# Feed-forward of a hybrid decoder block: down-projection terms behind later slots, and the last four down pages split whole into pages of their own

## The chip, the cores and the metric

One core of a Trainium2 chip runs the whole program. The metric is the device time of one execution in microseconds; the median of three runs is compared. One further execution was profiled, and all rows below come from it.

## The reference, cut to what matters

One decoder layer on x of 256 rows by 1024 columns, float32: a mixer (attention branches, gates, an output projection) and then a feed-forward part. The change is in the feed-forward part:

```python
h = rms_norm(x, norm_ffn_pre_g[l])
f = (jax.nn.silu(h @ w_gate[l]) * (h @ w_up[l])) @ w_down[l]
x = x + rms_norm(f, norm_ffn_post_g[l])
```

w_gate and w_up are 1024 x 2816, w_down is 2816 x 1024. In blocks of 128 there are 22 feed-forward blocks f and two row tiles t of 128 rows.

## The kernel before

**Products in three matmuls.** Every float32 factor is split into a high part (ScalarE copies it to a shorter float, line 183) and a low part (VectorE subtracts, line 186), and a product is three matmuls, high by high, high by low, low by high (`mm3`, lines 213 to 217). A weight granule is a page of 128 x 1024; its split takes one ScalarE and one VectorE instruction when it is done whole, and two of each when it is done in halves (`split_part`, `job_split`). Its parts are `whi` and `wlo` from a ring of five buffers (WB), or, for names in `place`, pages of their own (`wextra`). Raw weights land in a ring of seven tiles (`wraw`, RB) or, for the W units, in numbered pages (`wpage`).

**Units.** The first four blocks (NAT) are computed directly: gate, then up in eight slots (`nat_slots`). The other eighteen come in six UNITS by turns: R units of two blocks, at 4, 10 and 16, and W units of four blocks, at 6, 12 and 18. An R unit has eight slots, four granules by two row tiles. A W unit computes four blocks by a scheme with seven products instead of eight: granules 21, 11, T2, T1, T3, 22, T4, two slots each. Its T granules are sums of weight pages (`job_add`, line 267, VectorE): T3, T1 and T2, two halves each, are the six early sums (`early_sums`), done during the R unit before; T4 comes in the W unit. The T slots use S, sums of the activations that VectorE and ScalarE make once in nine steps (`s_step`). All slots here have six matmuls of 512 columns or as much.

**From f to the output.** When a unit's activations are done (`done`, line 1115 and 1117, in R; `q1` to `q7`, lines 1058 to 1091, in W), `f_T` transposes them on TensorE (line 992) into the PSUM bank t, ScalarE copies the high part of fT (line 997), and one slot later VectorE subtracts the low part (line 999). The bank t has one buffer, so the next transposes wait for that subtraction. Each f then gives two down-projection slots (`z_slots`), whose matmuls accumulate in `acc` and `pv`. The terms of a unit's blocks stand in the unit after it. The last four blocks, 18 to 21, are the tail: `z_tail` makes four slots for row tile 0 and four for row tile 1, and norm and output follow.

**What sets the order.** Three things, all in program order. First, the list `slots` (from line 1142): in each unit the first part a, the transposes `left` of the unit before, the part b, the down slots `zs` of the unit before, the part c. For R these are slots 1 to 2, 3 to 4 and 5 to 8; for W 21, then 11, then T2 to T4 and the transposes of row tile 0. In the last unit two of the four down slots stand after c. Second, the list of `jobs` (lines 244 to 330), splits and sums in the order in which ScalarE and VectorE do them. Third, `run` (line 338): before each slot it emits all jobs up to the last one that the slots ahead need, at most six slots ahead and at most four new granules (`granules_ahead`, line 353). Work after a slot (`post`, and steps of `active`) is emitted between, so activations queue behind the splits that were emitted before them. SP issues each load when its ring tile or page is released (`load_raws`), in order too. Pages are handed out first freed, first used (`free`).

**The tail before.** The splits of granules 18 to 21 are eight halves, first all first halves, then all second halves (line 328); 18 and 19 go into the ring, 20 and 21 into four free pages (`in_free`, line 853).

Of the kernel before, what the change touches and what calls it, by code (L numbers as in the profile page):

```python
# [21 lines left out]
F32R = mybir.dt.float32r  # L22
# [5 lines left out]
P = 128  # L28
D = 1024
S = 256  # L30
NT = S // P
# [4 lines left out]
NFF = DFF // P  # L36
# [29 lines left out]
def tile_hybrid_block(  # L66
# [182 lines left out]
            extra.append((("gn", kc), HALF[j]))  # L249
    for kc in range(2, 4):  # L250
        job_split(("gn", kc), nr["gn", kc], (0, 1))
    for kc in range(4):
        job_split(("un", kc), nr["un", kc], None if kc else (0, 1))

# [26 lines left out]
    def units_before(i):  # L283
# [4 lines left out]
        kb, fb = UNITS[i - 1]  # L288
        return list(range(fb, fb + (4 if kb == "W" else 2)))

    for ui, (kind, f0) in enumerate(UNITS):
        ds = [lambda i=i: job_split(("d", i), dr[i]) for i in units_before(ui)]
        if kind == "R":
            rr = [raw_of([(slice(0, 256), rows(w_gate, 2 * kc * P, 2, f0 * P, 256)),
                          (slice(256, 512), rows(w_up, 2 * kc * P, 2, f0 * P, 256))], 2) for kc in range(4)]
            rs = [lambda kc=kc: job_split(("r", f0, kc), rr[kc]) for kc in range(4)]
            ad = early_sums(UNITS[ui + 1][1])
            if ui == 0:
                sjobs = [raw_of([], 2, "page") for i in range(4)]

                def s_jobs(*ns):
                    def f():
                        if ns[0] == 0:
                            touch_s()
                        for n in ns:
                            add_job(lambda n=n: s_step(n))
                    return [f]

                def touch_s():
                    use(*sjobs)  # L310

                todo = s_jobs(0) + rs[0:1] + s_jobs(1) + rs[1:2] + s_jobs(2, 3) + ds[0:1] + s_jobs(4, 5) + ds[1:2] + \
                    s_jobs(6) + ds[2:3] + s_jobs(7, 8) + ds[3:4] + ad[0:1] + rs[2:3] + ad[1:3] + rs[3:4] + ad[3:]
            else:
                n = len(ds)
                todo = rs[0:2] + [x for i in range(n) for x in ds[i:i + 1] + ad[i:i + 1]] + rs[2:3] + ad[n:n + 1] + \
                    rs[3:4] + ad[n + 1:]
        else:
            b = wsum[f0]
            sp = {n: [lambda n=n, i=i: job_split((n, f0, i), b[n][i]) for i in range(2)]  # L320
                  for n in ("11", "21", "22", "T1", "T2", "T3", "T4")}
            t4 = [lambda i=i: job_add(b["T4"][i], b["T2"][i], b["21"][i]) for i in range(2)]
            todo = sp["21"] + sp["11"] + ds[0:1] + t4[0:1] + ds[1:2] + t4[1:2]
            for n in ("T2", "T1", "T3", "22", "T4"):
                todo += sp[n]
        for f in todo:
            f()
    for h in range(2):
        for f in range(NFF - NTAIL, NFF):
            job_split(("d", f), dr[f], (h,))  # L330

# [19 lines left out]
    def granules_ahead(slots, n, most):  # L353

        def f(i):
            j, seen = i + 1, set()
            while j < len(slots) and j - i <= most:
                seen |= {x for x, _ in slots[j]["need"]} - {x for x, _ in slots[i]["need"]}
                if len(seen) > n:
                    break  # L360
                j += 1
            return j - i - 1
        return f
# [184 lines left out]
    def ev_q(base):  # L548
        def f(c, a):
            q = work.tile([P, S], F32, tag="qf", name="q", bufs=2)  # L550
            nc.vector.tensor_tensor(q, a, R1, op=OP.mult)  # L551
            qhl = work.tile([P, 2, S], F32R, tag="q", name="q", bufs=5)
            qT[base + c] = (qhl[:, 0, :], qhl[:, 1, :])
            split(q, *qT[base + c])
        return f
# [294 lines left out]

    place[("z", 7)] = z7
    place[("gn", 0)], place[("gn", 1)] = in_pages(10, 11), in_pages(12, 13)
    for f in range(NFF - 2, NFF):
        place[("d", f)] = in_free

    sig(0)
# [128 lines left out]
    def f_T(fvs, f0, n, tag="t"):  # L985

        def pe():
            b = ps(tag)
            w = [(i, t, j) for i, t in enumerate(fvs) for j in range(n)]
            for i, t, j in w:  # L990
                c = (i * n + j) * P
                nc.tensor.transpose(b[:, c:c + P], fvs[t]()[:, j * P:(j + 1) * P], ident)
            h, l = [work.tile([P, 512], F32R, tag="q", name="fT", bufs=5) for _ in range(2)]
            for i, t, j in w:
                c = (i * n + j) * P
                fT[f0 + j, t] = [v[:, c:c + P] for v in (h, l)]
            nc.scalar.activation(h, b, AF.Copy)
            yield
            nc.vector.tensor_tensor(l, b, h.bitcast(F32), op=OP.subtract)  # L999

        def start():
            th = pe()
            next(th)
            active.append(th)
        return dict(pe=start, need=[], short=True)
# [36 lines left out]
    def unit_W(f0):  # L1042
        st = {}

        def bank(n):
            if n not in st:
                st[n] = ps("s")
            return st[n]

        def slots_of(n, bk, a, start, stop, post):  # L1050
            return [dict(pe=lambda kp=kp: block(bank(bk), a, n, f0, kp, start, stop), need=[((n, f0, kp), 0)],
                         post=[lambda: active.append(post())] if kp else []) for kp in range(2)]

        def q2():
            return
            yield

        def q1():
            s1 = work.tile([P, 512], F32, tag="ph0", name="s1", bufs=1)
            nc.scalar.activation(s1, st["a"], AF.Copy)  # L1060
            yield
            g = st["g0"] = work.tile([P, 512], F32, tag="e", name="g0", bufs=4)
            nc.vector.tensor_tensor(g, st["b"], s1, op=OP.add)
            yield
            nc.scalar.activation(g, g, AF.Silu, scale=rs2[:, 0:1])

        def q6():
            st["s2"] = work.tile([P, 512], F32, tag="ph0", name="s2", bufs=1)
            nc.scalar.activation(st["s2"], st["a"], AF.Copy)
            yield  # L1070

        def q5():
            st["v5"] = work.tile([P, 512], F32, tag="pl0", name="v5", bufs=1)
            nc.scalar.activation(st["v5"], st["b"], AF.Copy)
            yield

        def q7():
            nc.vector.tensor_tensor(st["v5"], st["v5"], st["a"], op=OP.subtract)  # L1078
            yield

        def q3():
            u = st["f0"] = work.tile([P, 512], F32, tag="e", name="f0", bufs=4)
            nc.vector.tensor_tensor(u, st["b"], st["s2"], op=OP.subtract)
            nc.vector.tensor_tensor(u, u, st["g0"], op=OP.mult)
            yield

        def q4():
            g = st["f1"] = work.tile([P, 512], F32, tag="e", name="f1", bufs=4)
            nc.scalar.activation(g, st["a"], AF.Silu, scale=rs2[:, 1:2])
            yield  # L1090
            nc.vector.tensor_tensor(g, g, st["v5"], op=OP.mult)

        head = slots_of("21", "b", A(0, 1), True, True, q2)
        body = slots_of("11", "a", A(0, 0), True, True, q1), [
            s for x in (("T2", "a", R_(1), False, True, q6), ("T1", "b", R_(0), True, True, q5),
                        ("T3", "a", R_(2), False, True, q7), ("22", "b", R_(3), False, True, q3),
                        ("T4", "a", A(1, 1), False, True, q4)) for s in slots_of(*x)]
        body[1].append(f_T({0: lambda: st["f0"]}, f0, 4))
        return head, body[0], body[1], [f_T({1: lambda: st["f1"]}, f0, 4)]

    def unit_R(f0):
        st = []
# [10 lines left out]
        def done(t):  # L1113
# [4 lines left out]

        sl = [dict(pe=lambda kc=kc, t=t: pe(kc, t), need=[(("r", f0, kc), 0)],
                   post=[lambda t=t: active.append(done(t))] if kc == 3 else []) for kc in range(4) for t in range(NT)]  # L1120
        return sl[0:2], sl[2:4], sl[4:8], [f_T({t: (lambda t=t: st[t]["f"]) for t in range(NT)}, f0, 2)]

    def nat_slots():
        def pe(kc, t):
# [20 lines left out]
        slots[t - NT]["post"] = [lambda t=t: nat_mul(t)]  # L1145
    left = [f_T({t: lambda t=t: fgs[t]}, 0, 4, "pv" if t else "t") for t in range(NT)]
    for i, (kind, f0) in enumerate(UNITS):
        a, b, c, nxt = unit_W(f0) if kind == "W" else unit_R(f0)
        zs = [s for f in units_before(i) for s in z_slots("d", f, f_of, NFF - 1)]
        if i == len(UNITS) - 1:  # L1150
            slots += a + left + b + zs[0:2] + c + zs[2:4] + nxt
        else:
            slots += a + left + b + zs + c
        left = nxt
    tail = list(range(NFF - NTAIL, NFF))
    t0 = z_tail("d", tail, f_of, 0, NFF - 1)
    t1 = z_tail("d", tail, f_of, 1, NFF - 1)
# [17 lines left out]
    t1[1]["post"] = [lambda: norm3(1)]  # L1175
    t1[2]["post"] = [lambda: pn[1][0](1)]
    t1[3]["post"] = [lambda: finish(1)]
    slots += t0 + t1
    run(slots, granules_ahead(slots, WB - 1, 6))
    order.__exit__(None, None, None)  # L1180

# [22 lines left out]
```

## Time and profile before

| | |
|---|---|
| median of 3 runs | 400.02 us (399.06 to 400.92) |
| profiled execution | 402.57 us |
| its span | 400.8 us |
| mean granted TensorE clock | 0.982 of full |
| VectorE, ScalarE busy | 78%, 59% of the span |
| feed-forward slots, from the first up-projection matmul to the last matmul | about 203 to 394.7 us of the span |

The profiled execution lies above the three runs. Times of rows are microseconds from the span's start. A matmul's end is modelled, so the shown idle time ahead of a matmul is counted from that end; the distance of two starts counts all of it.

### The profile page before, as it was taken

The page shows a single profiled execution, that of the slowest core. Times are in us where ns is not written, and L with a number is a line of the kernel's source. Part 1 is how long each engine was busy: PE and PEld are TensorE (multiplying, and loading weights), DVE is VectorE, ACT ScalarE, POOL GpSimd, SP SyncE. Part 2 cuts the span into 40 slices and gives each one's busy share as a digit, 9 for nine tenths or more (in the row PEclk, how much of TensorE's full clock was granted, in tenths as well). Part 3 has the DMA queues.
Part 4 walks back from the last instruction along what each step waited for, and adds up shares of the span by engine and source line. Part 5 has one row for each costly group of instructions (what it writes and reads, how often), then busy time and mean ns, then how long its engine had stood idle before and what let it go on. Part 6 is the DMA issues. An engine that isn't in the chain of part 4 may idle for free.

```text
span 400.8 us, 6146 instructions
## 1 busy us (share of the span) xinstructions
PE 376.9 (94%) x2212; PEld 326.6 (81%) x2212; DVE 312.0 (78%) x556; ACT 235.6 (59%) x435; POOL 31.5 (8%) x51
## 2 busy tenths in 40 slices
PE   6999999999999999999999898998989989979693
PEld 4799989999999999998888677877868868756583
DVE  2699787999987577895787999689786898668724
ACT  3875675787665855653693455854465554628411
POOL 0099500000001000000000000000000000000000
PEclk9899999999999999999999999999999999989979
DMA  6969655252545744783399836666464753000002
GB/s 193 389 218 328 199 177 164 71 187 88 172 145 160 253 134 141 251 267 111 115 330 341 279 111 194 200 216 186 138 202 135 235 194 121 0 0 1 2 1 105
DMA packets 37857, 67.65 MB, mean 169 GB/s; under 512 B 2993, under 2 KB 15298, under 8 KB 37826
## 3 DMA queue, kind: packets, MB, share of 16 engines
q1 hardware_dynamic: 37826, 67.26, 51.4%
q8 instruction: 17, 0.28, 0.3%
q14 instruction: 14, 0.11, 0.1%
HBM read 66.20 MB, written 1.05 MB: 168 GB/s over the span
## 4 chain that ended last, share of the span: by engine, by line
PE 75%; DVE 11%; issue 5%; DMA 4%; ACT 4%; SPq 1%; DVEq 0%; POOLq 0%; ACTq 0%
PE acc L217 13%; PE acc L215 12%; PE acc L216 12%; PE s L215 7%; PE s L216 7%; PE s L217 7%; DVE wlo L186 5%; PE acc L612 4%; DMA wraw<-in_w_in_dram 3%; ACT whi L183 2%; PE pv L216 2%; PE pv L217 2%; PE pv L215 2%; DVE wpage L267 2%; DVE fT L999 1%
## 5 line engine op out<-in xcount | busy, mean ns | idle before, releaser
L186 DVE TENSOR_TENSOR wlo<-wraw,whi 128x512 fp32r<-128x512 f32 (+1 forms) x141 | 119.2, 868 | 29.4 <-ACT whi L183 29.1
L183 ACT ACTIVATE whi<-wraw 128x512 fp32r<-128x512 f32 (+1 forms) x140 | 101.6, 763 | 43.4 <-PE acc L216 14.5
L215 PE MATMUL acc<-hTh,whi 128*128 128x256 f32 x256 | 73.2, 286 | 0.4 <-DVE q L551 0.4
L217 PE MATMUL acc<-hTh,wlo 128*128 128x256 f32 x256 | 71.9, 281 | 0.0
L216 PE MATMUL acc<-hTl,whi 128*128 128x256 f32 x256 | 71.8, 281 | 0.0
L186 DVE TENSOR_TENSOR wlo<-wpage,whi 128x1024 fp32r<-128x1024 f32 x42 | 50.0, 1220 | 18.5 <-ACT whi L183 18.5
L183 ACT ACTIVATE whi<-wpage 128x1024 fp32r<-128x1024 f32 x42 | 43.5, 1058 | 29.3 <-PE pv L217 18.8
L215 PEld LDWEIGHTS acc<-hTh,whi 128*128 128x128 f32 x256 | 48.3, 189 | 0.7 <-DVE q L551 0.6
L216 PEld LDWEIGHTS acc<-hTl,whi 128*128 128x128 f32 x256 | 48.3, 189 | 0.0
L217 PEld LDWEIGHTS acc<-hTh,wlo 128*128 128x128 f32 x256 | 48.2, 188 | 0.0
L215 PE MATMUL s<-whi,h2h 128*128 128x512 f32 x92 | 37.6, 409 | 0.9 <-DVE v L1078 0.6
L217 PE MATMUL acc<-whi,fT 128*128 128x512 f32 (+1 forms) x80 | 30.6, 382 | 7.6 <-DVE fT L999 7.6
L216 PE MATMUL s<-wlo,h2h 128*128 128x512 f32 x92 | 36.4, 396 | 0.0
L217 PE MATMUL s<-whi,h2l 128*128 128x512 f32 x92 | 36.4, 395 | 0.0
L215 PE MATMUL acc<-whi,fT 128*128 128x512 f32 (+1 forms) x80 | 30.1, 377 | 0.0
L216 PE MATMUL acc<-wlo,fT 128*128 128x512 f32 (+1 forms) x80 | 30.0, 375 | 0.0
L267 DVE TENSOR_TENSOR wpage<-wpage 128x1024 f32<-128x1024 f32 x24 | 28.9, 1216 | 0.0
L217 PEld LDWEIGHTS acc<-whi,fT 128*128 128x128 f32 x80 | 15.6, 195 | 12.7 <-DVE fT L999 10.2
L215 PEld LDWEIGHTS s<-whi,h2h 128*128 128x128 f32 x92 | 17.3, 188 | 6.0 <-DVE fr L1117 1.6
L875 POOL TENSOR_TENSOR rs_r<-rs_e,mhalf 128x1 f32<-128x1 f32 x4 | 2.2, 546 | 241.1 <-DVE rs_e L874 241.1
L217 PEld LDWEIGHTS s<-whi,h2l 128*128 128x128 f32 x92 | 17.3, 188 | 4.2
L216 PEld LDWEIGHTS s<-wlo,h2h 128*128 128x128 f32 x92 | 17.3, 188 | 3.4
(267 smaller groups left out, 768.5 us busy)
## 6 DMA issues: line engine op xcount, KB each, us to landing
wraw<-in_w_in_dram SPq DMA_DIRECT2D x37, 512.0 KB, 4.9
wraw<-in_w_down_dram SPq DMA_DIRECT2D x22, 512.0 KB, 3.4
wpage<-in_w_up_dram SPq DMA_DIRECT2D x12, 512.0 KB, 4.1
wpage<-in_w_gate_dram SPq DMA_DIRECT2D x12, 512.0 KB, 4.1
wraw<-in_w_out_dram SPq DMA_DIRECT2D x8, 512.0 KB, 3.3
wraw<-in_w_gate_dram SPq DMA_DIRECT2D x12, 256.0 KB, 2.9
wraw<-in_w_up_dram SPq DMA_DIRECT2D x12, 256.0 KB, 3.9
wraw<-in_w_branch_a_dram SPq DMA_DIRECT2D x4, 512.0 KB, 4.3
```

What stands on the lines that cost most here:

```text
L183: nc.scalar.activation(hi, src, AF.Copy)
L186: nc.vector.tensor_tensor(lo, src, hi.bitcast(F32), op=OP.subtract)
L215: nc.tensor.matmul(dst, lh, rh, start=start, stop=False, **kw)
L216: nc.tensor.matmul(dst, lh, rl, start=False, stop=False, **kw)
L217: nc.tensor.matmul(dst, ll, rh, start=False, stop=stop, **kw)
L267: nc.vector.tensor_tensor(dst["flat"], a["flat"], b["flat"], op=OP.add)
L612: nc.tensor.matmul(acc[t], l[:, k, ts_], r, start=k == 0 and n == 0, stop=k == KT - 1 and n == 2)
L875: nc.gpsimd.tensor_tensor(r[:, 0:1], e, mhalf, op=OP.pow)
L999: nc.vector.tensor_tensor(l, b, h.bitcast(F32), op=OP.subtract)
```

## The change

The up-projection splits 1 to 3 move from the list of early jobs into the first unit, by turns with the S steps. In an R unit the six slots 3 to 8 follow the transposes `left` at once; then come three down slots, the R unit's own transposes `tr`, and the other down slots. In a W unit the down slots follow 21 and 11. The jobs are put in the same order: in an R unit splits of r and d by turns with the early sums (`braid`); in the first unit the two T2 sums (`rest`) wait until the W unit. The last four down granules are split whole, in order, and all four go into eight free pages; granules with a place of their own no longer count for the four granules of look-ahead. In the tail the last transposes come after the first of the eight slots. The ring tagged q has six buffers instead of five.

```diff
@@ -249,8 +249,7 @@
-    for kc in range(4):
-        job_split(("un", kc), nr["un", kc], None if kc else (0, 1))
+    job_split(("un", 0), nr["un", 0], (0, 1))
@@ -287,6 +286,23 @@
+    def braid(a, b):
+
+        n, o = len(a), []
+        for i in range(n):
+            o += a[i:i + 1] + b[len(b) * i // n:len(b) * (i + 1) // n]
+        return o
@@ -296,38 +312,25 @@
             ad = early_sums(UNITS[ui + 1][1])
             if ui == 0:
...
-                todo = s_jobs(0) + rs[0:1] + s_jobs(1) + rs[1:2] + s_jobs(2, 3) + ds[0:1] + s_jobs(4, 5) + ds[1:2] + \
-                    s_jobs(6) + ds[2:3] + s_jobs(7, 8) + ds[3:4] + ad[0:1] + rs[2:3] + ad[1:3] + rs[3:4] + ad[3:]
+                uns = [lambda kc=kc: job_split(("un", kc), nr["un", kc]) for kc in range(1, 4)]
+                todo = uns[0:1] + s_jobs(0) + uns[1:2] + s_jobs(1) + uns[2:3] + s_jobs(2, 3, 4, 5) + rs[0:2] + \
+                    s_jobs(6) + rs[2:3] + s_jobs(7, 8) + rs[3:4] + braid(ds, ad[0:4])
+                rest = ad[4:]
             else:
-                n = len(ds)
-                todo = rs[0:2] + [x for i in range(n) for x in ds[i:i + 1] + ad[i:i + 1]] + rs[2:3] + ad[n:n + 1] + \
-                    rs[3:4] + ad[n + 1:]
+                todo = braid(rs + ds, ad)
+                rest = []
...
-            todo = sp["21"] + sp["11"] + ds[0:1] + t4[0:1] + ds[1:2] + t4[1:2]
+            todo = sp["21"] + sp["11"] + rest[0:1] + ds[0:1] + t4[0:1] + rest[1:2] + ds[1:2] + t4[1:2]
...
-    for h in range(2):
-        for f in range(NFF - NTAIL, NFF):
-            job_split(("d", f), dr[f], (h,))
+    for f in range(NFF - NTAIL, NFF):
+        job_split(("d", f), dr[f])
@@ -355,7 +358,7 @@
-                seen |= {x for x, _ in slots[j]["need"]} - {x for x, _ in slots[i]["need"]}
+                seen |= {x for x, _ in slots[j]["need"] if x not in place} - {x for x, _ in slots[i]["need"]}
@@ -549,7 +552,7 @@
-            qhl = work.tile([P, 2, S], F32R, tag="q", name="q", bufs=5)
+            qhl = work.tile([P, 2, S], F32R, tag="q", name="q", bufs=6)
@@ -850,7 +853,7 @@
-    for f in range(NFF - 2, NFF):
+    for f in range(NFF - NTAIL, NFF):
         place[("d", f)] = in_free
@@ -990,7 +993,7 @@
-            h, l = [work.tile([P, 512], F32R, tag="q", name="fT", bufs=5) for _ in range(2)]
+            h, l = [work.tile([P, 512], F32R, tag="q", name="fT", bufs=6) for _ in range(2)]
@@ -1096,7 +1099,7 @@
-        return head, body[0], body[1], [f_T({1: lambda: st["f1"]}, f0, 4)]
+        return head + body[0], body[1], [f_T({1: lambda: st["f1"]}, f0, 4)]
@@ -1118,7 +1121,7 @@
-        return sl[0:2], sl[2:4], sl[4:8], [f_T({t: (lambda t=t: st[t]["f"]) for t in range(NT)}, f0, 2)]
+        return sl, [f_T({t: (lambda t=t: st[t]["f"]) for t in range(NT)}, f0, 2)]
@@ -1145,13 +1148,14 @@
     for i, (kind, f0) in enumerate(UNITS):
-        a, b, c, nxt = unit_W(f0) if kind == "W" else unit_R(f0)
         zs = [s for f in units_before(i) for s in z_slots("d", f, f_of, NFF - 1)]
-        if i == len(UNITS) - 1:
-            slots += a + left + b + zs[0:2] + c + zs[2:4] + nxt
+        if kind == "R":
+            sl, tr = unit_R(f0)
+            slots += sl[0:2] + left + sl[2:] + zs[0:3] + tr + zs[3:]
+            left = []
         else:
-            slots += a + left + b + zs + c
-        left = nxt
+            a, b, left = unit_W(f0)
+            slots += a + zs[0:2] + (zs[2:] + b if i < len(UNITS) - 1 else b + zs[2:])
@@ -1175,7 +1179,7 @@
-    slots += t0 + t1
+    slots += t0[0:1] + left + t0[1:] + t1
```

## Rows read from the trace of the kernel before

**Rows 1.** Part 1 of the page: busy time, share of the span, instructions.

```profile
PE 376.9 (94%) x2212; PEld 326.6 (81%) x2212; DVE 312.0 (78%) x556; ACT 235.6 (59%) x435; POOL 31.5 (8%) x51
```

**Rows 2.** Timeline at the second wait for fT: start, length, instruction, idle before.

```profile
245.91 0.40 PE L215 MATMUL acc<-whi,fT 128*128 128x512 f32 x1
246.14 0.40 PE L216 MATMUL acc<-wlo,fT 128*128 128x512 f32 x1
...
246.90 0.68 DVE L999 TENSOR_TENSOR fT<-t,fT 128x512 fp32r<-128x512 f32 x1
...
247.64 0.50 PE L217 MATMUL acc<-whi,fT 128*128 128x512 f32 x1 [1.10 <-DVE fT L999]
...
247.98 0.40 PE L215 MATMUL acc<-whi,fT 128*128 128x512 f32 x1
```

**Rows 3.** Waits of TensorE in 214 to 395 us: total, times, longest.

```profile
PE acc L217 <- DVE fT L999: 7.6, 6, 2.6
PE t L992 <- DVE fT L999: 5.4, 3, 3.5
PE s L215 <- DVE v L1078: 0.6, 1, 0.6
PE s L215 <- DVE fr L1117: 0.4, 1, 0.4
```

**Rows 4.** Timeline ahead of the longest wait for fT, TensorE, VectorE and ScalarE.

```profile
347.69 0.69 PE L992 MATMUL t<-ident,fr 128*128 128x128 f32 x4
347.81 1.22 DVE L267 TENSOR_TENSOR wpage<-wpage 128x1024 f32<-128x1024 f32 x1
...
348.85 0.58 ACT L997 ACTIVATE fT<-t 128x512 fp32r<-128x512 f32 x1
...
351.21 2.35 DVE L186 TENSOR_TENSOR wlo<-wpage,whi 128x1024 fp32r<-128x1024 f32 x2
...
353.48 0.68 DVE L999 TENSOR_TENSOR fT<-t,fT 128x512 fp32r<-128x512 f32 x1
...
354.22 0.50 PE L217 MATMUL acc<-whi,fT 128*128 128x512 f32 x1 [2.58 <-DVE fT L999]
```

**Rows 5.** Busy time by stretch: window, its us, engines (instructions), granted clock, DMA.

```profile
214.00:380.00 166.00, 152.22 (x709) 121.74 (x707) 136.21 (x140) 91.97 (x109) 0.00 (x0) 0.99 0.46 146
...
355.00:359.00 4.00, 4.00 (x15) 3.42 (x14) 0.30 (x1) 1.00 (x1) 0.00 (x0) 0.57 0.00 0
380.00:386.20 6.20, 5.91 (x17) 4.80 (x18) 0.93 (x2) 0.60 (x1) 0.00 (x0) 0.52 0.00 0
```

**Rows 6.** Timeline of the tail, TensorE and VectorE.

```profile
371.02 0.69 DVE L1084 TENSOR_TENSOR f<-f,g 128x512 f32<-128x512 f32 x1
...
373.41 0.60 PE L992 MATMUL t<-ident,f 128*128 128x128 f32 x4
...
375.33 1.29 DVE L186 TENSOR_TENSOR wextra<-wraw,wextra 128x512 fp32r<-128x512 f32 x2 [2.42 <-ACT wextra L183]
...
376.51 0.28 PE L217 MATMUL pv<-whi,fT 128*128 128x256 f32 x1
...
379.56 0.68 DVE L999 TENSOR_TENSOR fT<-t,fT 128x512 fp32r<-128x512 f32 x1
380.29 1.12 PE L992 MATMUL t<-ident,f 128*128 128x128 f32 x4 [3.50 <-DVE fT L999]
```

**Rows 7.** Timeline of TensorE in the second stretch of low clock.

```profile
382.06 0.63 PE L217 MATMUL acc<-whi,fT 128*128 128x512 f32 x1
...
382.49 0.63 PE L215 MATMUL acc<-whi,fT 128*128 128x512 f32 x1
```

**Rows 8.** A page load, the sum that uses it, and part 6 of the page.

```profile
288.84 3.20 SPq L164 DMA_DIRECT2D wpage<-in_w_up_dram  x2
...
323.75 1.22 DVE L267 TENSOR_TENSOR wpage<-wpage 128x1024 f32<-128x1024 f32 x1
...
wpage<-in_w_up_dram SPq DMA_DIRECT2D x12, 512.0 KB, 4.1
```

**Rows 9.** Waits of ScalarE in 214 to 395 us: total, times, longest.

```profile
ACT whi L183 <- PE pv L217: 23.9, 12, 5.2
```

More of the change, by code (lines that the diff above doesn't have):

```diff
@@ L289, in units_before, with s_jobs, f @@
         return list(range(fb, fb + (4 if kb == "W" else 2)))
+    sjobs = [raw_of([], 2, "page") for i in range(4)]
+    def s_jobs(*ns):
+        def f():
+            if ns[0] == 0:
+                use(*sjobs)
+            for n in ns:
+                add_job(lambda n=n: s_step(n))
+        return [f]
+    def braid(a, b):
[3 more added lines that the diff above has]
+        return o
     for ui, (kind, f0) in enumerate(UNITS):
@@ L298, in tile_hybrid_block @@
             if ui == 0:
[L299 to L310, printed above, removed]
-                todo = s_jobs(0) + rs[0:1] + s_jobs(1) + rs[1:2] + s_jobs(2, 3) + ds[0:1] + s_jobs(4, 5) + ds[1:2] + \
-                    s_jobs(6) + ds[2:3] + s_jobs(7, 8) + ds[3:4] + ad[0:1] + rs[2:3] + ad[1:3] + rs[3:4] + ad[3:]
-            else:
-                n = len(ds)
-                todo = rs[0:2] + [x for i in range(n) for x in ds[i:i + 1] + ad[i:i + 1]] + rs[2:3] + ad[n:n + 1] + \
-                    rs[3:4] + ad[n + 1:]
+                uns = [lambda kc=kc: job_split(("un", kc), nr["un", kc]) for kc in range(1, 4)]
+                todo = uns[0:1] + s_jobs(0) + uns[1:2] + s_jobs(1) + uns[2:3] + s_jobs(2, 3, 4, 5) + rs[0:2] + \
+                    s_jobs(6) + rs[2:3] + s_jobs(7, 8) + rs[3:4] + braid(ds, ad[0:4])
+                rest = ad[4:]
+            else:
+                todo = braid(rs + ds, ad)
+                rest = []
         else:
```

## Prediction

> **What bounds the kernel now.** I read the page first, then the waits of TensorE, the timeline at the waits, and the timeline of VectorE just ahead of them. The page shows TensorE busy for 94% of the span [rows 1], and where nothing waits a 128x512 matmul starts every 0.23 us [rows 2]. So time can only come from stretches where matmuls stop or where the clock is low. The feed-forward stage from 214 to 395 us has both. Its waits [rows 3] are six for the low part of fT at the first down-projection matmul that needs it (7.6 us), three at the transposes (5.4 us, the longest 3.5) and two small ones (0.6 and 0.4 us).
>
> Why fT is late is seen on VectorE. In the worst case the copy of the high part is done at 349.4, one microsecond after the transposes, but VectorE, which works in order, has 2 sums and 3 splits queued ahead of the subtraction that makes the low part, and runs them without a gap from 347.81 to 353.48 [rows 4]. The two slots between the transposes and the first term give it only 2.8 us. VectorE is not full: in 214 to 380 us it is busy 136.2 of 166 us [rows 5]. The work stands in the wrong order.
>
> **The sum, step by step.** It is made against the profiled execution: 402.57 us, a span of 400.8 and 1.8 around it. That is 2.55 above the median of the runs shown, 400.02, and above the highest of them.
>
> 1. Down-projection terms later. In a unit of kind R the transposes stay behind slot 2, but six projection slots of 1.40 us (six matmuls of 0.233), not two, now stand between them and the first term: 8.4 us instead of 2.8. In a unit of kind W the own transposes of the R before it come after three term slots, and five term slots and four slots of the unit follow: 12.6 us. The latest low part in [rows 4] comes 6.4 us after its transposes begin (347.69 by the matmul chain, 354.16 by the end of the subtraction), so both covers hold, and all six waits go. Their size: the view counts idle from a modelled end, 0.40 us after the start, while the stream starts one every 0.233, so each costs 0.17 more (246.14 to 247.64 is 1.50, that is 1.27 lost for 1.10 shown), and the next start after a wait takes 0.34 instead of 0.23 [rows 2]: 7.6 + 6 x 0.17 + 6 x 0.1 = 9.2 us.
>
> 2. The R unit's multiply. The last R slots were followed by the W unit, whose bank they hold (0.4 us shown [rows 3]); now the term slots stand between. With the same two corrections 0.7 us goes.
>
> 3. The tail. Now the eight half splits of the last four pages stand on ScalarE behind the silu that waits for the last T4 matmul, and on VectorE six of them, 3.8 us, ahead of the multiply and the subtraction for which the transposes at 380.29 wait [rows 6]. After the change the four whole splits need no buffer of the ring of five, look-ahead no longer counts them, and they are emitted up to six slots ahead. The transposes also move behind the first tail slot, 1.4 us. The wait of 3.5 goes; by starts it is 3.78 less 0.12: 3.7 us. Half splits cost two of 0.61 each on VectorE, whole ones 1.13 [rows 4, 6], which is hidden work and worth nothing.
>
> 4. What the tail pays. Two whole splits, 2.3 us, come to stand ahead of the two multiplies that make f0. The second of these ran at 371.02, so the f0 transposes at 373.41 had 1.7 us to spare (371.71 to 373.41) [rows 6]. So these wait 0.6, with the restart 0.7 us. Two more splits, the last multiply and the subtraction then end at 374.0 + 2.3 + 0.6 + 0.7 = 377.6 on the old clock, while the third matmul of the first tail slot comes 0.6 + 2.8 + 0.5 after 374.0, at 377.9: it just holds, 0.3 us to spare. Bounds of this step: 0 if the splits go still earlier, 3.0 if all four stand ahead.
>
> 5. The clock. The granted clock is 0.57 of full in 355 to 359 us and 0.52 in 380 to 386.2 [rows 5], which is the lower level, 1.2 GHz, for nearly all of it; matmuls then start every 0.43 us instead of 0.233 [rows 7]. Ahead of each fall TensorE had stood, for 2.58 us (to 354.22, [rows 4]) and for 3.5; in the stretch of the other five waits, 5.0 us together, the mean stays high enough (0.99 to 380 us with the first fall in it) for no third fall. With steps 1 and 3 both go. Low from 355.24 to 358.7 and from 380.3 to 386.1: 9.3 us, of which (0.43 - 0.233) / 0.43 = 46% is lost: 4.2 us, 1.5 and 2.7. The Trainium skill, "TensorE: Matmul & The Clock Gate", Part 1 and its terms, says that the throttled state is the default which activity lifts, and that the loss is the throttled time by one minus the ratio; by it this term would be 4.7 instead of 4.2. The trace agrees on the direction.
>
> 6. Edits costed at nothing. The first unit's `un` splits, the S steps and the last two T2 sums only change order: VectorE does the same number of splits and sums. In the first 22 us after 203 TensorE has eight up-projection and eight R slots, 22.4 us, and VectorE's three `un`, four r splits and four whole S steps (11 x 1.13) plus four half ones and two multiplies (6 x 0.6) are 16.0 us. For a later pair R and W: 24 splits and 8 sums at 1.13 and some 10 small ones come to 42 us, TensorE's 204 matmuls of 512 columns and 12 transposes to 49. That is the cover, 7 us a pair; if it is gone, rival (a) has the price. A sixth q buffer only adds room. POOL has nothing to do in the stage [rows 5]. On SP's queue the ring loads of `un` and r now precede the d loads, and the two 21 pages precede T2, which is no load; pages are issued early: the pair at 288.84 is used by the sum at 323.75 [rows 8]. The other two waits at the transposes, (5.4 - 3.5) / 2 = 0.95 us each, keep what stands ahead of them, a split and the multiply ahead of the subtraction, and stay, as does the 0.6 at T4 [rows 3].
>
> Sum: 9.2 + 0.7 + 3.7 + 4.2 - 0.7 = **17.1 us**. From the profiled time 385.5. From the median 382.9 if all runs have these losses, more if the 2.55 us by which the profiled one is longer are part of the low clock. I take the middle, **384.5 us**.
>
> **Rivals.** (a) VectorE becomes the bound. Its 29.8 us of idle time in 214 to 380 [rows 5] must shrink to some 17. For it: VectorE is dense for 6.4 us in [rows 4], and the tail has 0.3 us to spare. Against: the cover of step 6. If only half can be squeezed, half the sum comes: about 392.5 us.
>
> (b) The ring of five split buffers is what makes fT late. ScalarE waits 23.9 us, 12 times, for a down-projection matmul to free one [rows 9]. Then moving slots leaves the six waits and the first low-clock stretch where they are, and only the tail (3.7 + 2.7 - 0.7 = 5.7) comes: 401.3, the middle of median and profiled time, less 5.7, 395.5 us. The Trainium skill, "Perfetto Trace Analysis", Optimization Strategy, holds that the same gap repeating on the engine that should be full can mean too few buffers. Against: ahead of the latest subtraction VectorE waited for nothing for 5.7 us [rows 4].
>
> (c) The tail doesn't come early, because the eight free pages that its splits need are freed by this same unit's splits of 11, T2, T1 and T3. Pages are handed out first freed first, and between the split that frees the last of them, T3, and the one that takes it stand the four of 22 and T4 and three of the tail, some 8 us of VectorE at 1.13 each, so I hold it unlikely. The price is steps 3 and 4 and the second low stretch: 384.5 + 5.7, about 390 us.
>
> (d) Slower: a sum blocked on a page load. From the second R unit on, sums follow the second r split at once; on an engine in order a sum that waits for its page holds all splits and fT behind it. A page takes 4.1 us from issue to landing [rows 8]. It decides from five such waits on (5 x 4.1 is over 17.1); with all eight sums of one R and W pair (six early, two T4), 33 us less 17, it gives some 417 us. Against: the 30 us lead of [rows 8].
>
> **How the numbers follow.** My forecast has a chance of 0.72, (a) 0.12, (c) 0.08, (b) 0.05, (d) 0.03. The range 381.5 to 391 holds the forecast with its unknowns (the median taken whole, and up to 3 us for step 4, and 4.2 for the clock) and (c), and leaves out (b), (d) and most of (a). A measurement here can tell about 0.5%, 2 us, from no change. All cases but (d) are faster by more, with a little left for several small mishaps: 0.95 faster, 0.02 the same, 0.03 slower.
>
> **What would show it.** Right: the wait of the down-projection for fT is gone from TensorE's waits, that at the transposes is near 2.5 us, with one of 0.6 near the end; the granted clock is 1.0 from the stage's begin to the last matmul; VectorE's idle time in the stage is about 17 us; wextra is split in four whole pairs ahead of the last f0 multiply. Wrong: matmuls that wait for wlo (a), the fT wait still there (b), the last transposes still waiting over 2 us (c), sums that wait for a DMA (d), or the low clock at another place.

## The result, and the profile after

The changed kernel takes **383.69 us** (median of 4, 383.51 to 383.90) against 400.25 for the kernel before: 16.6 us less, a ratio of 0.959 with a 95% interval of 0.957 to 0.961. The forecast was 384.5 in a range of 381.5 to 391.

The profiled execution of the changed kernel takes 383.57 us with a span of 381.8, which is 19.0 below the profiled execution before. Of these, 17.3 lie between the first feed-forward matmul on h2 and the last matmul (190.90 to 394.43 before, 189.19 to 375.42 after). The other 1.7 lie ahead of the feed-forward part, where the change does nothing of note: the profiled execution before had a low clock in its first 20 us (mean 0.91 by its windows, 1.00 after). It fits that this is part of the 2.55 us by which it lay above the median.

TensorE's waits after the change, to be held against [rows 3] (total, times, longest; 214 to 376 us):

```profile
PE t L995 <- DVE fT L1002: 1.9, 2, 1.0
PE s L215 <- DVE v L1081: 0.6, 1, 0.6
PE t L995 <- DVE f L1087: 0.6, 1, 0.6
PE s L215 <- DVE g L1066: 0.2, 1, 0.2
```

The first row of [rows 3], 7.6 us for fT at the down-projection, is gone, and so is the R unit's multiply. The two waits at the transposes and the one at T4 are what the prediction left standing. The third row here is the price that step 4 named; the fourth, 0.2 us for g in a W unit, is new and was not forecast.

The page's first part and its clock line (granted clock in 40 slices):

```profile
PE 369.8 (97%) x2212; PEld 323.1 (85%) x2212; DVE 311.1 (81%) x552; ACT 233.7 (61%) x431; POOL 31.6 (8%) x51
...
PEclk9999999999999999999999999999999999999998
```

Busy time in the stage, with the granted clock, which answers to [rows 5]:

```profile
214.00:366.00 152.00, 148.69 (x713) 121.38 (x712) 132.15 (x131) 88.29 (x104) 0.00 (x0) 1.00 0.49 159
```

About the same work (713 matmul instructions, 709 before) takes 14 us less, the granted clock of the window is 1.00, and VectorE's idle time fell from 29.8 to 19.9 us, not quite to the 17 that the prediction gave as a sign. From 190 us to the last matmul no stretch has a low clock either (mean 1.00). The subtraction that makes the low part of fT now has room to spare. After the last R unit, TensorE, VectorE and TensorE again:

```profile
328.56 0.60 PE L995 MATMUL t<-ident,fr 128*128 128x128 f32 x4
...
328.76 1.22 DVE L266 TENSOR_TENSOR wpage<-wpage 128x1024 f32<-128x1024 f32 x1
...
329.90 2.35 DVE L186 TENSOR_TENSOR wlo<-wpage,whi 128x1024 fp32r<-128x1024 f32 x2
332.17 0.68 DVE L1002 TENSOR_TENSOR fT<-t,fT 128x512 fp32r<-128x512 f32 x1
...
342.02 0.39 PE L217 MATMUL acc<-whi,fT 128*128 128x512 f32 x1
```

VectorE still has work queued ahead of the subtraction, one sum and two splits where [rows 4] has two and three, and the low part is done 4.3 us after the transposes begin, not 6.5. But the matmul that needs it comes 13.5 us after them, 9.2 us after the low part is done (332.17 + 0.68 to 342.02). So two things changed, the queue and the place of its reader. The later place is enough by itself on these numbers: even behind a W unit's transposes the first matmul that can need the low part comes 9.4 us after they begin (265.68 to 275.04), which is over the old 6.5. The shorter queue alone is not quite enough: in the order before, the reader would have come 3.8 us after the transposes without its wait (354.22 - 2.58 - 0.17 - 347.69), half a microsecond before 4.3. No run tried the two apart.

The tail, which answers to [rows 6], with ScalarE's copies of the four pages:

```profile
354.75 3.90 ACT L183 ACTIVATE wextra<-wraw 128x1024 fp32r<-128x1024 f32 x4
...
356.81 2.36 DVE L186 TENSOR_TENSOR wextra<-wraw,wextra 128x1024 fp32r<-128x1024 f32 x2
...
359.81 0.69 DVE L1087 TENSOR_TENSOR f<-f,g 128x512 f32<-128x512 f32 x1
360.41 2.35 DVE L186 TENSOR_TENSOR wextra<-wraw,wextra 128x1024 fp32r<-128x1024 f32 x2
...
360.64 0.63 PE L995 MATMUL t<-ident,f 128*128 128x128 f32 x4 [0.55 <-DVE f L1087]
...
363.29 0.68 DVE L1002 TENSOR_TENSOR fT<-t,fT 128x512 fp32r<-128x512 f32 x1
...
364.35 0.40 PE L217 MATMUL acc<-wextra,fT 128*128 128x512 f32 x1
```

On VectorE two whole splits stand ahead of the f0 multiplies and two behind them, as step 4 said; the prediction's sign, all four pairs ahead of the last f0 multiply, came on ScalarE alone. The f0 transposes wait 0.55 us (0.6 forecast), and the low part is done at 363.97, 0.4 us ahead of the matmul that needs it (0.3 forecast).

### The profile page after: what moved, and what is told of

It reads as the page before. It is cut to its first block, busy times and chain, and to the rows that moved or that the text cites. A ratio compares the mean times of both kernels' runs of the same rounds, so it can differ in the third digit from the quotient of the medians.

```text
span 381.8 us, 6133 instructions
## 1 busy us (share of the span) xinstructions
PE 369.8 (97%) x2212; PEld 323.1 (85%) x2212; DVE 311.1 (81%) x552; ACT 233.7 (61%) x431; POOL 31.6 (8%) x51
## 4 chain that ended last, share of the span: by engine, by line
PE 89%; DVE 5%; issue 2%; ACT 2%; DMA 1%; SPq 1%; DVEq 0%; POOLq 0%; ACTq 0%
PE acc L215 14%; PE acc L217 14%; PE acc L216 14%; PE s L215 9%; PE s L216 9%; PE s L217 9%; PE acc L615 6%; PE pv L216 2%; PE pv L217 2%; PE pv L215 2%; DVE wlo L186 2%; DMA xt<-in_x_dram 1%; ACT whi L183 1%; PE t L995 1%; PE t L216 1%
## 5 line engine op out<-in xcount | busy, mean ns | idle before, releaser
L186 DVE TENSOR_TENSOR wlo<-wraw,whi 128x512 fp32r<-128x512 f32 (+1 forms) x137 | 116.7, 873 | 29.3 <-ACT whi L183 28.9
L183 ACT ACTIVATE whi<-wraw 128x512 fp32r<-128x512 f32 (+1 forms) x136 | 99.1, 766 | 37.1 <-PE acc L216 14.4
L215 PE MATMUL acc<-whi,fT 128*128 128x512 f32 x72 | 26.5, 369 | 0.0
L217 PE MATMUL acc<-whi,fT 128*128 128x512 f32 x72 | 26.2, 364 | 0.0
L216 PE MATMUL acc<-wlo,fT 128*128 128x512 f32 x72 | 26.1, 363 | 0.0
L215 PEld LDWEIGHTS s<-whi,h2h 128*128 128x128 f32 x92 | 17.3, 188 | 4.7 <-ACT wextra L183 1.0
L217 PEld LDWEIGHTS s<-whi,h2l 128*128 128x128 f32 x92 | 17.3, 188 | 4.3
L216 PEld LDWEIGHTS s<-wlo,h2h 128*128 128x128 f32 x92 | 17.3, 188 | 3.6
L215 PE MATMUL s<-whi,S 128*128 128x512 f32 x48 | 19.2, 399 | 0.3 <-DVE g L1066 0.2
```

Of the source, the lines that this page charges most:

```text
L183: nc.scalar.activation(hi, src, AF.Copy)
L186: nc.vector.tensor_tensor(lo, src, hi.bitcast(F32), op=OP.subtract)
L215: nc.tensor.matmul(dst, lh, rh, start=start, stop=False, **kw)
L216: nc.tensor.matmul(dst, lh, rl, start=False, stop=False, **kw)
L217: nc.tensor.matmul(dst, ll, rh, start=False, stop=stop, **kw)
```

## The experiments

Each was timed beside the kernel before, whose median was 399.83 us beside the runs with the order, the tail, the zeros and the later transposes, and, on another chip, 399.24 beside the next four and 400.19 beside the last two. The changed kernel was not timed again beside them: what is said against its 383.69 compares runs of different times, and a few tenths can't be told. One order timed on both chips gave 381.66 and 381.80.

### The order without the tail, and the tail without the order

The first keeps the new order and takes the tail back:

```diff
-    for f in range(NFF - NTAIL, NFF):
-        job_split(("d", f), dr[f])
+    for h in range(2):
+        for f in range(NFF - NTAIL, NFF):
+            job_split(("d", f), dr[f], (h,))
...
-seen |= {x for x, _ in slots[j]["need"] if x not in place} - ...
+seen |= {x for x, _ in slots[j]["need"]} - ...
...
-    for f in range(NFF - NTAIL, NFF):
+    for f in range(NFF - 2, NFF):
         place[("d", f)] = in_free
...
-    slots += t0[0:1] + left + t0[1:] + t1
+    slots += left + t0 + t1
```

> The changed kernel with the tail as it was before: eight half splits, two of the four tail pages in the ring of five, look-ahead counting all granules, the last transposes ahead of the tail. Only the order of slots and jobs in the units is new. My theory (low parts queued behind other VectorE work, and clock): steps 1 and 2 and the first low-clock stretch come, 9.2 + 0.7 + 1.5 = 11.4 us, so about 388.9 against 400.25; the six waits for fT are gone, the tail wait of 3.5 us and the low clock after it stay. If the ring of five buffers made fT late, nothing in the ring has changed, the six waits stay and the time is 400. If VectorE is the bound, matmuls wait for wlo instead and the gain is half, 394 to 395.

Measured: **388.34 us** (387.79 to 390.34), ratio 0.972 (0.968 to 0.975), 11.5 us less than before. Its waits of TensorE in the stage:

```profile
PE t L996 <- DVE fT L1003: 5.4, 3, 3.5
PE s L215 <- DVE v L1082: 0.6, 1, 0.6
PE s L215 <- DVE g L1067: 0.2, 1, 0.2
```

The six waits are gone with the ring of five split buffers as it was, so rival (b) falls: these buffers were not what made fT late. (The sixth q buffer is in this run too; the last run below has five, and the six waits are gone there as well.) Matmuls don't wait for wlo, so VectorE isn't the bound either. The tail wait of 3.5 stays, and its profile has the low clock behind it (0.72 and 0.50 in 366 to 370 us).

The second is the kernel before with the same lines the other way round, and with the last transposes taken out of the last unit's slots.

> The kernel before with the new tail alone: four whole splits in pages of their own, not counted by look-ahead, and the last transposes behind the first tail slot. My theory: steps 3 and 4 and the second low-clock stretch, 3.7 + 2.7 - 0.7 = 5.7 us, so about 394.5; the f0 transposes near the end wait 0.6 us, the six waits for fT and the first low-clock stretch stay. If the pages come free too late, the last transposes still wait over 2 us and the time is 399 to 400.

Measured: **395.93 us** (394.67 to 396.06), ratio 0.989 (0.986 to 0.991): 3.9 us, not 5.7. The waits are as expected:

```profile
PE acc L217 <- DVE fT L998: 7.7, 6, 2.6
PE t L991 <- DVE fT L998: 1.9, 2, 1.0
...
PE t L991 <- DVE f L1083: 0.6, 1, 0.6
```

So the part in waits, 3.7 less 0.7, came, and rival (c) falls: the pages are free in time. What is missing is put down to the clock, and this is not shown. It fits: three of the four executions (395.88 to 396.06) have a mean clock of 0.991, the profiled one of them with the fall after the longest fT wait, and the fourth, 394.67, has 0.995; the kernel before, by the next run, need not have both falls in its median. The two halves together give 11.5 + 3.9 = 15.4 of the 16.6; each works without the other.

### The clock by itself

The kernel before, with matmuls of zeros while TensorE would stand in the tail:

```diff
-slots += a + left + b + zs[0:2] + c + zs[2:4] + nxt
+slots += a + left + b + zs[0:2] + c + zs[2:4] + [dict(pe=lambda: keep_warm(28, ps("s")), need=[], short=True)] + nxt
```

> The kernel before with 28 extra matmuls of zeros, 256 columns, into a spare bank while TensorE would stand before the last transposes. The wait itself is set by VectorE and keeps its length. If the low clock after 380 us comes from TensorE standing there, the matmuls after it now start every 0.23 us instead of 0.43 and 2.7 us go: about 397.5. If the low clock has another cause, no change: 400.2, or up to 0.5 us slower by the extra matmuls.

Measured: **397.29 us** (396.46 to 398.10), ratio 0.993 (0.990 to 0.996), 2.5 us less, by doing more. Its timeline at the place of [rows 6] and [rows 7]:

```profile
375.39 3.23 PE L412 MATMUL s<-warm 128*128 128x256 bf16 x28
378.46 0.60 PE L992 MATMUL t<-ident,f 128*128 128x128 f32 x4
...
379.59 0.40 PE L215 MATMUL acc<-whi,fT 128*128 128x512 f32 x1
379.82 0.39 PE L216 MATMUL acc<-wlo,fT 128*128 128x512 f32 x1
```

Nothing but TensorE's standing was changed, and the matmuls behind it start every 0.23 us instead of 0.43. All four executions lie below all seven of the kernel before timed beside them (399.32 to 401.11). The low clock of the tail comes from that standing, where it comes. The four runs also fall in pairs: 398.10 and 397.99 with a mean clock of 0.992, 396.46 and 396.59 with 0.996 and 0.997. The profile, of the first of these, has the low clock after the longest wait for fT, at 352.6 us; a difference of 1.5 us is just what that stretch costs in the profile before. It fits that this fall comes in some executions only; the others weren't profiled. The kernel before points the same way: of its 25 executions on the other chip six took 396.96 to 397.95 with a mean clock of 0.997, the other nineteen 398.79 to 401.53 with 0.986 to 0.995. So the same standing seems to bring the low clock in most executions and not in all.

### What was left over: transposes two slots later

```diff
-            slots += sl[0:2] + left + sl[2:] + zs[0:3] + tr + zs[3:]
+            slots += sl[0:4] + left + sl[4:] + zs[0:3] + tr + zs[3:]
```

> The changed kernel with the transposes of row tile 1 of a W unit two slots later in the R unit that follows (behind slot 4, not slot 2). My theory: the two waits of 0.95 us that stay in the changed kernel are for the low part of row tile 0, which frees the bank; 2.8 us more between the two hide it, and four slots, 5.6 us, still hide the next low part. By starts each is 1.1 us longer than none, with the restart 1.2: 2.4 us, about 381.3 against 383.7. If the later low part is late then, the down-projection waits again and nothing is gained: 383.7 or more.

Measured: **381.66 us** (381.51 to 382.37), ratio 0.954 (0.952 to 0.956), 2.0 us under the changed kernel. Both waits at the transposes are gone from its profile.

### The place of the last transposes

The changed kernel with `slots += left + t0 + t1`.

> The changed kernel with the last transposes ahead of the first tail slot again, all else as changed. My theory: the early whole splits do the work of the tail, and the place of the transposes is worth little. The low part that frees their bank ends at 363.97 in the changed kernel's profile and they would stand at 363.89, so they wait some 0.1 to 0.7 us: 383.8 to 384.4 against 383.7. If the place is what hides the wait of 3.5 us, a slot's 1.4 us or more comes back, 385 and up, with the low clock perhaps 387.5.

Measured: **384.08 us** (383.84 to 384.35). The waits at the transposes are three, 2.7 us together, so this one is 0.8, a little over the range given for it. The early splits do the work; the place saves 0.8 us of waits in the profile and some 0.4 us of time, which is at the edge of what can be told.

### How much room VectorE has

```diff
                 todo = braid(rs + ds, ad)
+                todo = braid(todo, [lambda: add_job(lambda: nc.vector.tensor_tensor(zgs[0], xt[:, 0, :], xt[:, 0, :], op=OP.add))] * 4)
```

and the same with 12.

> The changed kernel with 4 extra sums of 128x1024 on VectorE, read by nobody, spread over the jobs of each of the second and third R units (8 in all, 9 us of VectorE). My theory: VectorE has 7 us to spare in a pair of R and W, 4 x 1.13 = 4.5 us fit, no change: 383.7 to 384.2. If VectorE is already the bound in the changed kernel, all 9 us show: about 392.7.

Measured: **383.96 us** (383.55 to 385.58). Nine microseconds more of VectorE cost nothing that can be told.

> The same with 12 extra sums in each of the two R units (13.6 us of VectorE each). My theory: 13.6 less the 7 to spare, so 6.6 us come out of each pair, 13 us in all: about 397. If VectorE is already the bound: 383.7 + 27 = 411. If its room is larger than counted: below 390.

Measured: **399.84 us** (399.59 to 400.37, 10 runs), 16.1 over the changed kernel, 3 more than forecast. Its waits and two windows:

```profile
PE t L996 <- DVE fT L1003: 5.4, 2, 3.0
PE t L996 <- DVE fr L1121: 3.4, 2, 2.4
PE s L216 <- DVE wlo L186: 2.5, 2, 1.5
```

```profile
262.00:276.00 14.00, 11.60 (x48) 9.09 (x47) 14.00 (x14) 5.56 (x7) 0.00 (x0) 0.88 0.38 125
334.00:346.00 12.00, 9.58 (x44) 7.82 (x43) 12.00 (x14) 5.17 (x7) 0.00 (x0) 0.86 0.39 132
```

Its three longest waits of TensorE:

```profile
267.68 0.66 PE L996 MATMUL t<-ident,f 128*128 128x128 f32 x4 [2.40 <-DVE fT L1003]
325.09 0.65 PE L996 MATMUL t<-ident,f 128*128 128x128 f32 x4 [2.98 <-DVE fT L1003]
340.78 1.11 PE L996 MATMUL t<-ident,fr 128*128 128x128 f32 x4 [2.42 <-DVE fr L1121]
```

VectorE is busy without a gap in the two windows, so here it is the bound, and every kind of its work is waited for. The clock falls again, which the expectation had left out, behind the waits of 2.40 and 2.42 us and not behind the longest, 2.98 (mean granted clock 1.00 in 325 to 337 us): the length of a wait alone does not tell whether a fall comes. The loss is 14 x 0.12 + 12 x 0.14, some 3.4 us, and all ten executions have a mean clock of 0.984 to 0.990. What is left, 12.7, agrees with the 13 worked out from a room of 7 us a pair; this split of the 16.1 was made after the run. Rival (a) was real as a mechanism, and the changed kernel is not in it.

### The price of step 4 taken away

Transposes two slots later as above, and look-ahead paced for the tail granules:

```diff
+    reach = {("d", f): 5 if f < NFF - 2 else 2 for f in range(NFF - NTAIL, NFF)}
...
-            while j < len(slots) and j - i <= most:
+            while j < len(slots) and j - i <= min([most] + [reach[x] for x, _ in slots[j]["need"] if x in reach]):
```

In the first version of this run the table's name, `late`, is bound again further down in the program, so nothing was paced. It gave 381.80 us (381.65 to 381.98), a repeat of the run with late transposes.

> The changed kernel with the transposes of row tile 1 behind slot 4 of the R unit (as in the run before, 381.66), and look-ahead for the tail granules cut to five slots for the first two and two slots for the last two, so that on VectorE the first two splits come behind the multiplies of f0 and the last two behind the last low part of f0. My theory: step 4's price, the wait of 0.6 with its restart, goes: 381.0. If the splits are then late for the tail slots, matmuls of the tail wait for wextra and it is 382 or more.

> The paced tail once more: in the run before, the name of its table was bound again further down in the program, so that the order of VectorE stayed as it was and the run repeats the late transposes alone (381.8 and 381.66). Now the limit holds. Expected as then: the 0.6 wait of the f0 transposes goes with its restart, 0.7 us, so about 381.0, and the splits lie behind the f0 multiplies and behind the low part of f0; or, if matmuls of the tail wait for wextra then, 382 or more.

Measured: **380.99 us** (380.59 to 381.54, 6 runs), ratio 0.954 (0.950 to 0.957). The tail:

```profile
356.25 0.69 DVE L1089 TENSOR_TENSOR f<-f,g 128x512 f32<-128x512 f32 x1
356.86 2.36 DVE L186 TENSOR_TENSOR wextra<-wraw,wextra 128x1024 fp32r<-128x1024 f32 x2
...
358.64 0.60 PE L997 MATMUL t<-ident,f 128*128 128x128 f32 x4
...
360.17 0.69 DVE L1004 TENSOR_TENSOR fT<-t,fT 128x512 fp32r<-128x512 f32 x1
360.99 2.36 DVE L186 TENSOR_TENSOR wextra<-wraw,wextra 128x1024 fp32r<-128x1024 f32 x2
```

The multiplies now run ahead of the first two splits, the low part ahead of the last two, and the f0 transposes at 358.64 wait for nothing. This version is 2.7 us under the changed kernel.

### The sixth q buffer

`bufs=6` back to `bufs=5` in both places of the changed kernel.

> The changed kernel with five buffers tagged q instead of six. My theory: the sixth buffer was costed at nothing, 383.7. If a low part that is used later needs it, the copies to fT wait for a buffer and it is 384.5 or more.

Measured: **385.50 us** (385.46 to 385.90), 1.8 over the changed kernel: my theory falls. The subtraction that follows an R unit's own transposes now waits for a buffer. Its timeline row in the first R unit, and VectorE's waits of this kind:

```profile
236.01 0.69 DVE L1002 TENSOR_TENSOR fT<-t,fT 128x512 fp32r<-128x512 f32 x1 [2.98 <-PE acc L216]
```

```profile
DVE fT L1002 <- PE acc L216: 8.9, 3, 3.0
```

It happens once in each R unit. Two fT buffers, high and low, are live for each set of transposes, and with the terms moved later the third set comes while the first two are still being read. VectorE, in order, stands 3 us and everything behind it is late; TensorE feels some 1.8 us of it: 1.3 by the waits for v (1.1, twice, in place of 0.6, once), g (0.6 in place of 0.2) and wlo (0.4, new), and 0.5 by the starts of the two waits that are new, at 0.27 each as in step 1.

## Why the prediction was right, and where it was not

**Step 1**, 9.2 us for six waits, and **step 2**, 0.7: right. The order alone gave 11.5 us, against 9.9 and the clock. Both covers hold: 9.2 us are to spare behind the last R unit's transposes, and 4.3 or more behind a W unit's (low part done at 270.76, first reader at 275.04). The step took VectorE's queue as it was, 6.4 us, and left the shorter queue out.

**Steps 3 and 4**, 3.7 and -0.7: right. The tail alone has exactly the waits forecast. The 0.55 us at the transposes and the 0.4 us of margin on the low part came as worked out from durations of the rows before. In the tail the early splits carry it; moving the transposes is worth some 0.4 us. Which part of the early splits does it, whole splits, own pages or look-ahead, was not tried.

**Step 5**, 4.2 us of clock: the mechanism right, the size too large for the median. The zero matmuls show that standing lowers the clock. But the profiled execution seems to have more of it than others: the sum of 17.1 fits the 17.3 us between the two profiles, while the medians differ by 16.6 (16.1 to the median of the first four runs). Less the 12.9 us of waits that leaves 3.2 to 3.7 for the clock. The six executions of the kernel before with a mean clock of 0.997 lie 13.3 to 14.3 us above the changed kernel, near the 12.9 of the waits without any clock term. I took the middle between median and profiled time for this reason, but slipped: the middle of 385.5 and 382.9 is 384.2, not 384.5. The result lies 0.5 us below the first and 0.8 below the second. The term of 4.7 by the Trainium skill, "TensorE: Matmul & The Clock Gate", Terms, is farther off.

**Step 6** had one edit wrong: the sixth q buffer "only adds room". It is worth 1.8 us, and without it the change brings some 14.8 (400.25 to 385.50). The time forecast did not suffer, as the buffer was part of the change. The error was to move the readers of fT later without counting how many fT are then live. The rest held: VectorE's room of 7 us a pair is bounded from both sides (4 sums fit, 12 don't), and the `un` splits, S steps and T2 sums cost nothing that the profile shows.

**The rivals.** (a) falls by the run with 4 extra sums, (b) by the order alone, (c) by the tail alone. (d), a sum blocked on a page load, shows in no wait of VectorE in the changed kernel, and ScalarE waits for a page once, 0.3 us; it was not tried by itself. Nor was a larger ring, or the new slots with the old order of jobs.

## What to carry to other kernels

Where an engine that works in order makes something small behind a queue of large work, moving its reader later can be worth as much as shortening the queue: add up the queue ahead of it and put that much of the reader's other work between. Then count what stays live longer, and give the pool that buffer in the same edit. A wait on TensorE can have a second price in the clock behind it, here behind waits of 2.4 to 3.5 us but not behind every such wait, so a sum made on one profile should be held against the median with that in mind.

## What the runs showed of the hardware

28 matmuls that compute nothing made the kernel 2.5 us faster when they filled a wait of 3.5 us (397.29 against 399.83), about as expected. What was not expected is how unevenly the low clock comes. In one execution it came behind waits of 2.40 and 2.42 us and not behind one of 2.98. And executions of one kernel lie in groups that go with the mean clock (398.0 at 0.992 and 396.5 at 0.996 to 0.997 in the run with the zeros): this fits a fall that comes in one execution and not in the next, though each kernel was profiled once only.
